# Gate and up projections by seven block products in place of eight (Strassen) in a float32 decoder trunk

## The chip, the cores and the metric

The kernel runs on one core of one Trainium2 chip. The metric is the time of one execution on the device in microseconds (us). Below, PE is the matrix engine (TensorE), PEld its weight loads, DVE the vector engine, ACT the scalar engine, POOL GpSimd and SP the engine that issues most transfers.

## The reference

A trunk of two layers works on 512 tokens of width 1024, all in float32. Each layer is a feed-forward block, a mixer block and a second feed-forward block. With `h = rmsnorm(x) * gain`, a feed-forward block is

```
x = x + 0.5 * rmsnorm((silu(h @ wg) * (h @ wu)) @ wd)      # wg, wu: 1024 x 2816, wd: 2816 x 1024
```

The mixer projects `h` with one wide matrix, runs two kinds of attention and a causal convolution on slices of it, projects and gates the three results, adds them up and multiplies by `w_out`. Its arithmetic isn't touched by the change. There are four feed-forward blocks in all (two per layer).

## The kernel before

**Precision.** Each float32 operand of a matmul is split into two parts, `hi` (ACT copies it into the type float32r, line 119) and `lo` (DVE subtracts `hi` from the value, line 120). A product is then three matmuls into the same PSUM bank: lo x hi, hi x hi and hi x lo (`mm3`, lines 137 to 139). `hh` and `hl` are the two parts of the normalised and transposed tokens, `raw` is a loaded piece of a weight.

**Gate and up (in `ffn`).** The 2816 columns of the two matrices are cut into 22 chunks of 128, `NF = 22`. For each chunk, `col_chunks` loads 256 columns of `wg` and of `wu` at a time (1 MB each, two buffers `raw`), splits them, and `proj_group` runs 8 steps of the contraction x 3 matmuls with 512 token columns for gate and the same for up. Then ACT applies silu (line 290), DVE multiplies (291), and the product is split again (293 and 294) and kept for the down projection. The first two chunks are done by `proj_lead` in two halves of 256 tokens, so that PE can begin when half of the tokens are normalised.

**Down (`proj_out`).** For two halves of 512 output columns, 22 contraction steps x 4 token tiles x 3 matmuls with 512 columns. The last steps (`tail`: 8 in the second half) are ordered by token tile, so that the first tiles are complete early and their norm and the next stage's norm (`prenorm`: norm on ACT, DVE and POOL, transposes on PE, split on ACT and DVE) run while PE works on the last tiles. The split weights of that tail go to buffers of the feed-forward block (`slots`), not to the ring `hi`/`lo`, which has `HLB = 3` buffers each.

**Order.** Dependencies and buffers are followed by a scheduler at build time. It puts each engine's instructions into a fixed order: of those that can run, the one that comes first in the program. On the chip each engine goes through its list in that order. PSUM has eight banks of 512 float32 per partition, shared out as `pm` 3, `ps` 2, `pt` 2, `po` 1.

## Time and profile before

| | |
|---|---|
| Median of 3 runs | 2572.33 us (2569.75 to 2574.19) |
| Profiled execution, time | 2571.34 us |
| Its span in the trace | 2569.5 us |
| PE matmuls | 12,072 |
| DVE busy | 1247.5 us |
| ACT busy | 930.4 us |

The span is what the trace covers; the rest of the execution's time lies around it. Matmuls are pipelined, so that the duration of one is longer than the step from one start to the next; the steps are read from the starts. Busy time of the other engines is the time in which they execute. The granted clock is a column of the profile: 1.00 means 2.4 GHz.

### The profile page before, as it was taken

Reading aid. Unit: us, or ns where it says so; the run is one execution under the profiler, and the core shown is the slowest. Engines: PE = TensorE matmul, PEld = TensorE weight load, DVE = VectorE, ACT = ScalarE, POOL = GpSimd, SP = SyncE. Lnnn points to the kernel's source line nnn. Section 1 sums busy time; section 2 is a strip of 40 time slices with the busy share of each in tenths; the row PEclk is TensorE's granted clock in tenths of the full one; section 3 lists DMA queues with packets and bytes.
Section 4 is the critical chain, followed back from the end, with each engine's and each line's share of the span. In section 5 each row is a group of like instructions: output and inputs, shape, how many; then the busy total and the mean of one; then the engine's idle time right before and its main releaser. Section 6 shows DMA issues by size and latency. Waiting matters only on the chain.

```text
span 2569.5 us, 29966 instructions
## 1 busy us (share of the span) xinstructions
PE 2521.8 (98%) x12072; PEld 2101.8 (82%) x12072; DVE 1247.5 (49%) x1838; ACT 930.4 (36%) x1625; POOL 245.7 (10%) x156
## 2 busy tenths in 40 slices
PE   8999999999999999999999999999899999999999
PEld 7888888778787888888888888887788878888887
DVE  4333244796577453332443332446956765433323
ACT  4322244633524442222332222446235244422222
POOL 0000012160011110000000000130600101100000
PEclk9999999999999999999999999999999999999999
DMA  4323345242122422223322223452421224132232
GB/s 157 103 98 98 107 147 145 65 130 93 42 91 74 165 86 97 92 92 105 107 95 92 93 98 106 157 141 59 129 80 52 91 74 165 65 99 99 99 107 74
DMA packets 211820, 261.48 MB, mean 102 GB/s; under 512 B 8160, under 2 KB 167264, under 8 KB 211424
## 3 DMA queue, kind: packets, MB, share of 16 engines
q1 hardware_dynamic: 204000, 249.06, 29.6%
q10 hardware_dynamic: 7680, 10.50, 1.6%
q8 instruction: 95, 1.56, 0.2%
q14 instruction: 45, 0.37, 0.0%
HBM read 237.47 MB, written 6.29 MB: 95 GB/s over the span
## 4 chain that ended last, share of the span: by engine, by line
PE 92%; DVE 5%; issue 1%; ACT 1%; DMA 0%; ACTq 0%; SPq 0%; DVEq 0%
PE pm L137 23%; PE pm L138 23%; PE pm L139 23%; PE ps L138 2%; PE ps L139 2%; PE ps L137 2%; DVE y L363 2%; PE pt L138 2%; PE pt L139 2%; PE pt L137 2%; PE po L137 1%; PE po L138 1%; PE po L139 1%; DVE lo L120 1%; PE pt L487 1%
## 5 line engine op out<-in xcount | busy, mean ns | idle before, releaser
L137 PE MATMUL pm<-hh,lo 128*128 128x512 f32 (+1 forms) x2288 | 869.9, 380 | 3.2 <-DVE lo L120 3.2
L138 PE MATMUL pm<-hh,hi 128*128 128x512 f32 (+1 forms) x2288 | 868.8, 380 | 0.0
L139 PE MATMUL pm<-hl,hi 128*128 128x512 f32 (+1 forms) x2288 | 867.6, 379 | 0.0
L120 DVE TENSOR_TENSOR lo<-raw,hi 128x1024 fp32r<-128x1024 f32 x374 | 486.4, 1302 | 717.0 <-ACT hi L119 715.1
L119 ACT ACTIVATE hi<-raw 128x1024 fp32r<-128x1024 f32 x374 | 395.8, 1059 | 706.8 <-PE pm L139 349.5
L137 PEld LDWEIGHTS pm<-hh,lo 128*128 128x128 f32 x2288 | 431.3, 188 | 86.2 <-DVE lo L120 5.0
L139 PEld LDWEIGHTS pm<-hl,hi 128*128 128x128 f32 x2288 | 431.3, 189 | 79.9 <-issue 0.7
L138 PEld LDWEIGHTS pm<-hh,hi 128*128 128x128 f32 x2288 | 431.3, 188 | 79.6 <-issue 0.7
L363 DVE SCALAR_TENSOR_TENSOR y<-z,ppl,y 128x512 f32<-128x512 f32 x240 | 213.5, 890 | 4.2
L291 DVE TENSOR_TENSOR sg<-sg,pm 128x512 f32<-128x512 f32 (+1 forms) x88 | 59.5, 676 | 247.6 <-PE pm L139 215.5
L290 ACT ACTIVATE sg<-pm 128x512 f32<-128x512 f32 x88 | 51.6, 591 | 327.7 <-PE pm L139 327.7
L213 POOL TENSOR_TENSOR h<-x,gain 128x512 f32<-128x512 f32 x40 | 52.4, 1331 | 1159.4 <-DVE x L271 1131.8
L137 PE MATMUL pm<-hi,il 128*128 128x512 f32 x264 | 102.7, 389 | 0.0
L138 PE MATMUL pm<-hi,ih 128*128 128x512 f32 x264 | 102.7, 389 | 0.0
L139 PE MATMUL pm<-lo,ih 128*128 128x512 f32 x264 | 102.7, 389 | 0.0
L395 POOL TENSOR_TENSOR sw<-sw,cs 128x512 f32<-128x512 f32 x40 | 64.0, 1600 | 244.1 <-DMA sw<-raw 127.2
L479 DVE CUSTOM_DVE_ANT_0 s<-ps,cs 128x256 f32<-128x256 f32 (+3 forms) x128 | 56.2, 448 | 57.1 <-ACT st L489 17.5
L616 ACT ACTIVATE gt<-pm,late 128x512 f32<-128x512 f32 x40 | 27.6, 690 | 137.3 <-PE pm L139 137.3
L636 POOL TENSOR_TENSOR m<-gt 128x512 f32<-128x512 f32 x16 | 33.6, 2103 | 408.4 <-DVE gt L623 408.4
L137 PE MATMUL pm<-hi,hl 128*128 128x512 f32 (+1 forms) x144 | 53.9, 374 | 13.7 <-DVE qk L391 13.7
L384 ACT ACTIVATE raw<-pm 128x512 f32<-128x512 f32 x40 | 23.9, 598 | 105.3 <-PE pm L139 66.1
L294 DVE TENSOR_TENSOR il<-sg,ih 128x512 fp32r<-128x512 f32 x88 | 60.3, 685 | 3.4 <-ACT ih L293 3.4
(288 smaller groups left out, 3369.1 us busy)
## 6 DMA issues: line engine op xcount, KB each, us to landing
raw<-in_w_in_dram SPq DMA_DIRECT2D x62, 1024.0 KB, 5.4
raw<-in_ffn_w_gate_dram SPq DMA_DIRECT2D x43, 1024.0 KB, 5.0
raw<-in_ffn_w_up_dram SPq DMA_DIRECT2D x43, 1024.0 KB, 5.0
raw<-in_ffn_w_down_dram SPq DMA_DIRECT2D x40, 1024.0 KB, 4.7
sw<-raw ACTq DMA_DIRECT2D x160, 64.0 KB, 2.0
raw<-in_w_out_dram SPq DMA_DIRECT2D x8, 1024.0 KB, 4.7
raw<-in_ffn_w_down_dram SPq DMA_DIRECT2D x8, 512.0 KB, 3.3
xd<-x SPq DMA_DIRECT2D x16, 256.0 KB, 2.0
```

The lines of the kernel that those rows point to most:

```text
L119: S.activation(hi, raw, AF.Copy)
L120: last = V.tensor_sub(lo, raw, bc(hi))
L137: PE.matmul(ps, sl, mh, start=first, stop=False, skip_group_check=not check)
L138: PE.matmul(ps, sh, mh, start=False, stop=False, skip_group_check=not check)
L139: PE.matmul(ps, sh, ml, start=False, stop=last, skip_group_check=not check)
L213: G.tensor_mul(h[j], xs[t][:, j * T:(j + 1) * T], g[:, j * T:(j + 1) * T])
L290: S.activation(sg[:, c], pg, AF.Silu)
L291: V.tensor_mul(sg[:, c], sg[:, c], pu)
L294: V.tensor_sub(il, sg, bc(ih))
L363: V.scalar_tensor_tensor(y, z[:, j:j + T], cw[:, c, j:j + 1], y, op0=ALU.mult, op1=ALU.add)
L395: G.tensor_mul(sw, sw, sin)
L479: V.tensor_tensor_reduce(out=s, in0=ps, in1=mask, scale=1.0, scalar=3e38, op0=ALU.add, op1=ALU.min, accum_out=nm)
```

## The change

From the second pair of chunks on (`u` = 1 to 10), the 256 columns of gate and the 256 columns of up are handled as one matrix product. The contraction (1024) is cut into two halves and the tokens into two halves of 256; "rows" are the two halves of the pair of matrices, `wg` and `wu`. A 2x2 by 2x2 block product takes eight block products, and Strassen's scheme (in Winograd's form) takes seven. Each block product, `product`, is 2 column groups x 4 contraction steps x 3 matmuls with 256 token columns. The sums and differences that the scheme needs are formed by DVE: on the weight side `s1` to `s4` in each unit, on the token side four tiles `tt` once per block, before the first unit. Partial results are combined in PSUM: ACT copies a bank that holds a partial sum into another bank (`W`, `Vb`, `Y`), and the next product adds onto it. The last product of a unit, with `s4`, is issued in the next unit (`late`). The first unit is plain (`lead_unit`, the same 192 matmuls with 256 columns as `proj_lead`).

The gated product is kept unsplit, and `proj_out` splits it for the down projection, in each of its two halves. There, `slots` is None: the tail's weights go to the ring `hi`/`lo`, whose buffers go from 3 to 4 each, and the tail of the second half is 6 steps, not 8. In the first feed-forward block four matmuls and four ACT reads (`own`) are put ahead of the lead. `hh` and `hl` become two halves of one tile `hb`. `FUSE` is False, so the branches that it guards aren't built. The scratch space for dynamic transfers is set to 1024.

```diff
--- before.py
+++ after.py
@@ -33,7 +33,8 @@
 QA0, KA0, VA0 = 0, 768, 1536
 
 TAIL = 8
-HLB = 3
+HLB = 4
+FUSE = False
 ZRB = 6
 PRE_UP = 60
 CST = [("ident", 128), ("cos", 512), ("sin", 512), ("mc", 512), ("m0", 256), ("m12", 256)]
@@ -144,6 +145,32 @@
             for k in range(KD):
                 mm3(p_, wh[:, k, :], wl[:, k, :], hh[:, k, :], hl[:, k, :], k == 0, k == KD - 1)
         return ps
+
+    def lead_unit(wg, wu, hb, raws=None):
+        if raws is None:
+            raws = [load(w[:, 0:2 * P], KD, 2 * P) for w in (wg, wu)]
+        wts = {(f, j): split(raws[j][:, :, f * P:(f + 1) * P]) for f in range(2) for j in range(2)}
+        H = T // 2
+        whole = [bank("pm") for _ in range(2)]
+        parts = [bank("pt") for _ in range(2)]
+        for s in range(2):
+            c = slice(s * H, (s + 1) * H)
+            outs = [(whole[0], c, s == 0), (whole[1], c, s == 0),
+                    (parts[s], slice(0, H), True), (parts[s], slice(H, T), False)]
+            for (f, j), (z, d, first) in zip(((0, 0), (0, 1), (1, 0), (1, 1)), outs):
+                for k in range(KD):
+                    wh, wl = (w[:, k, :] for w in wts[f, j])
+                    m = hb[:, :, k, c]
+                    PE.matmul(z[:, d], wl, m[:, 0, :], start=first and k == 0, stop=False, skip_group_check=True)
+                    if FUSE:
+                        o = z.rearrange("p (a n) -> p a n", n=H)[:, d.start // H:d.start // H + 1, :]
+                        PE.matmul(o.to_broadcast([P, 2, H]), wh, m, start=False, stop=k == KD - 1,
+                                  skip_group_check=True)
+                    else:
+                        PE.matmul(z[:, d], wh, m[:, 0, :], start=False, stop=False, skip_group_check=True)
+                        PE.matmul(z[:, d], wh, m[:, 1, :], start=False, stop=k == KD - 1, skip_group_check=True)
+        return [[(slice(0, T), *whole)],
+                [(slice(s * H, (s + 1) * H), parts[s][:, 0:H], parts[s][:, H:T]) for s in range(2)]]
 
     def proj_lead(w, c0, c1, hh, hl, spare, raws=None):
         if raws is None:
@@ -198,11 +225,11 @@
         first = g is not None
         if g is None:
             g = bcast_row(row)
-        hh = per.tile([P, KD, T], F32R, tag="hh", name="hh")
-        hl = per.tile([P, KD, T], F32R, tag="hl", name="hl")
+        hb = per.tile([P, 2, KD, T], F32R, tag="hb", name="hb")
+        hh, hl = hb[:, 0], hb[:, 1]
         with tc.high_priority(offset=PRE_UP):
             prenorm_tiles(g, hh, hl, first)
-        return hh, hl
+        return hb
 
     def prenorm_tiles(g, hh, hl, first):
         for t in range(NT):
@@ -227,22 +254,23 @@
                 S.activation(dh, pt, AF.Copy)
                 V.tensor_sub(hl[:, 4 * j:4 * j + 4, t * P:(t + 1) * P], pt, bc(dh))
 
-    def proj_out(stat, slots, w, row, half_step):
-        K = len(stat)
+    def proj_out(K, stat, ntail, slots, w, row, half_step):
         g = bcast_row(row)
         ss = [[sp.tile([P, 1], F32, tag="ss", name="ss", bufs=8) for _ in range(2)] for _ in range(NT)]
         yg = []
         for half in range(2):
             ps = [bank(b_) for b_ in (("pm", "pm", "pm", "ps") if half == 0 else ("pt", "ps", "pt", "po"))]
             c0 = half * T
-            tail = K - (2 if half == 0 else len(slots))
-            parts = {}
+            tail = K - (2 if half == 0 else ntail)
+            parts, pairs = {}, {}
             for k0 in range(0, K, 4):
                 kn = min(4, K - k0)
                 raw = load(w[k0 * P:(k0 + kn) * P, c0:c0 + T], kn, T)
                 for s in range(0, kn, 2):
                     k = k0 + s
-                    if half == 0 or k < tail:
+                    for u in range(2):
+                        pairs[k + u] = stat(k + u)
+                    if slots is None or half == 0 or k < tail:
                         wh, wl = split(raw[:, s:s + 2, :])
                         for u in range(2):
                             parts[k + u] = (wh[:, u, :], wl[:, u, :])
@@ -253,7 +281,7 @@
                 if k0 + kn == K:
                     ops += [(k, t) for t in range(NT) for k in range(tail, K)]
                 for k, t in ops:
-                    sh, sl = stat[k]
+                    sh, sl = pairs[k]
                     wh, wl = parts[k]
                     mm3(ps[t], sh[:, t * P:(t + 1) * P], sl[:, t * P:(t + 1) * P], wh, wl, k == 0, k == K - 1)
             for t in range(NT):
@@ -271,34 +299,138 @@
                     V.scalar_tensor_tensor(xs[t][:, 0:T], yg[t], r, xs[t][:, 0:T], op0=ALU.mult, op1=ALU.add)
                     V.scalar_tensor_tensor(xs[t][:, T:D], y, r, xs[t][:, T:D], op0=ALU.mult, op1=ALU.add)
 
+    def product(dst, sw, mv, start):
+        for f in range(2):
+            for k in range(4):
+                c = slice(f * P, (f + 1) * P)
+                sh, sl = sw[0][:, k, c], sw[1][:, k, c]
+                m = mv[:, :, k, :]
+                PE.matmul(dst[:, f, :], sl, m[:, 0, :], start=start and f == 0 and k == 0, stop=False, skip_group_check=True)
+                if FUSE:
+                    PE.matmul(dst[:, f:f + 1, :].to_broadcast([P, 2, T // 2]), sh, m, start=False, stop=k == 3,
+                              skip_group_check=True)
+                else:
+                    PE.matmul(dst[:, f, :], sh, m[:, 0, :], start=False, stop=False, skip_group_check=True)
+                    PE.matmul(dst[:, f, :], sh, m[:, 1, :], start=False, stop=k == 3, skip_group_check=True)
+
     def ffn(pre, post, wg, wu, wd, early=None):
         gain, raws = early or (None, None)
-        hh, hl = prenorm(pre, gain)
+        H = T // 2
+        hb = prenorm(pre, gain)
         with tc.tile_pool(name="inner", bufs=1, reuse_waits="tile") as ip:
-            inner = []
-
-            def pair(f):
-                return tuple(ip.tile([P, T], F32R, tag=f"i{u}{f}", name="i" + u) for u in "hl")
-
-            spare = iter((NF - 1, NF - 2))
-            lead = proj_lead((wg, wu), 0, 0, hh, hl, lambda: pair(next(spare)), raws)
-            rest = ([(slice(0, T), *proj_group([gc[1], uc[1]], hh, hl))]
-                    for gc, uc in zip(col_chunks(wg, 256, FF), col_chunks(wu, 256, FF)))
-            for f, pieces in enumerate(chain(lead, rest)):
-                sg = sp.tile([P, T], F32, tag="t2k", name="sg", bufs=5)
-                for c, pg, pu in pieces:
-                    S.activation(sg[:, c], pg, AF.Silu)
-                    V.tensor_mul(sg[:, c], sg[:, c], pu)
-                ih, il = pair(f)
-                S.activation(ih, sg, AF.Copy)
-                V.tensor_sub(il, sg, bc(ih))
-                inner.append((ih, il))
-                if early and f == 5:
-                    lambdas()
-            proj_out(inner, [lambda f=f: pair(f) for f in range(TAIL)], wd, post, True)
+            inner = [ip.tile([P, 2, T], F32, tag=f"i{u}", name="inner") for u in range(NF // 2)]
+            t2k = lambda name: sp.tile([P, 2, H], F32, tag="t2k", name=name, bufs=5)
+            with tc.tile_pool(name="comb", bufs=1, reuse_waits="tile") as cp:
+                def comb(name):
+                    return cp.tile([P, 4, H], F32, tag="s", name=name, bufs=4)
+
+                def block(k, t):
+                    return hb[:, :, 4 * k:4 * k + 4, t * H:(t + 1) * H]
+
+                if early:
+                    own = [bank(tag) for tag in ("pm", "pm", "pm", "po")]
+                    for z in own:
+                        PE.matmul(z, hb[:, 0, 0, 0:P], hb[:, 0, 0, :], start=True, stop=True, skip_group_check=True)
+                    for z in own:
+                        S.activation(junk[0][:, 0:1], z[:, 0:1], AF.Copy)
+                lead = lead_unit(wg, wu, hb, raws)
+
+                b = {}
+                def added(k, t):
+                    b[k, t] = comb("b")
+                    z = block(k, t)
+                    V.tensor_add(b[k, t], bc(z[:, 0]), bc(z[:, 1]))
+
+                tt = {}
+                def tsplit(i, z):
+                    tt[i] = cp.tile([P, 2, 4, H], F32R, tag=f"t{i}", name="t")
+                    split(z, (tt[i][:, 0], tt[i][:, 1]))
+
+                fl = lambda z: z.rearrange("p a b -> p (a b)")
+                added(0, 0)
+                added(0, 1)
+                V.tensor_sub(fl(b[0, 0]), fl(b[0, 0]), fl(b[0, 1]))
+                added(1, 1)
+                V.tensor_sub(fl(b[0, 1]), fl(b[1, 1]), fl(b[0, 1]))
+                V.scalar_tensor_tensor(fl(b[1, 1]), fl(b[1, 1]), -1.0, fl(b[0, 0]), op0=ALU.mult, op1=ALU.subtract)
+                tsplit(6, b[1, 1])
+                tsplit(5, b[0, 0])
+                added(1, 0)
+                V.scalar_tensor_tensor(fl(b[1, 0]), fl(b[1, 1]), -1.0, fl(b[1, 0]), op0=ALU.mult, op1=ALU.subtract)
+                tsplit(4, b[1, 0])
+                tsplit(7, b[0, 1])
+                for f, pieces in enumerate(lead):
+                    for c, pg, pu in pieces:
+                        z = inner[0][:, f, c]
+                        S.activation(z, pg, AF.Silu)
+                        V.tensor_mul(z, z, pu)
+
+                def pbank(tag):
+                    return bank(tag, (P, 2, H))
+
+                late = []
+                for u in range(1, NF // 2):
+                    c0 = u * 2 * P
+                    rg, ru = [load(w_[:, c0:c0 + 2 * P], KD, 2 * P) for w_ in (wg, wu)]
+                    w11, w12, w21, w22 = rg[:, 0:4, :], rg[:, 4:8, :], ru[:, 0:4, :], ru[:, 4:8, :]
+                    X, W = pbank("ps"), pbank("pm")
+                    Vb, Y = pbank("pt"), pbank("pm" if u % 2 == 0 else "po")
+                    it = inner[u]
+                    s1, s2 = comb("s1"), comb("s2")
+                    o11 = split(w11)
+                    V.tensor_add(s1, w21, w22)
+                    V.tensor_add(s2, s1, w11)
+                    product(X, o11, block(0, 0), True)
+                    S.activation(W, X, AF.Copy)
+                    os2 = split(s2)
+                    for f_ in late:
+                        f_()
+                    late.clear()
+                    product(X, os2, tt[6], False)
+                    S.activation(Vb, X, AF.Copy)
+                    o12 = split(w12)
+                    s4, s3 = comb("s4"), comb("s3")
+                    V.tensor_add(s4, s2, w12)
+                    V.tensor_add(s3, w11, w21)
+                    product(W, o12, block(1, 0), False)
+                    g1 = t2k("g1")
+                    S.activation(g1, W, AF.Silu)
+                    os1 = split(s1)
+                    product(X, os1, tt[5], False)
+                    S.activation(Y, X, AF.Copy)
+                    o22 = split(w22)
+                    product(Vb, o22, tt[4], False)
+                    a2 = t2k("a2")
+                    V.tensor_copy(a2, Y)
+                    V.tensor_sub(a2, Vb, a2)
+                    os3 = split(s3)
+                    product(X, os3, tt[7], False)
+                    V.tensor_add(a2, a2, X)
+                    V.scalar_tensor_tensor(it[:, :, 0:H], a2, -1.0, g1, op0=ALU.mult, op1=ALU.mult)
+
+                    def finish(X=X, Y=Y, s4=s4, it=it, t2k=t2k):
+                        product(Y, split(s4), block(1, 1), False)
+                        g2 = t2k("g2")
+                        S.activation(g2, Y, AF.Silu)
+                        V.scalar_tensor_tensor(it[:, :, H:T], X, -1.0, g2, op0=ALU.mult, op1=ALU.mult)
+
+                    late.append(finish)
+                    if early and u == 2:
+                        lambdas()
+                late[0]()
+            with tc.tile_pool(name="pairs", bufs=1, reuse_waits="tile") as pp:
+                def stat(k):
+                    if k < 2:
+                        into = tuple(sp.tile([P, T], F32R, tag="h", name="i" + u, bufs=4) for u in "hl")
+                    else:
+                        into = tuple(pp.tile([P, T], F32R, tag="i" + u, name="i" + u, bufs=11) for u in "hl")
+                    return split(inner[k // 2][:, k % 2, :], into)
+
+                proj_out(NF, stat, TAIL - 2, None, wd, post, True)
 
     def mixer(l):
-        hh, hl = prenorm(a["mix_norm_pre"][l])
+        hb = prenorm(a["mix_norm_pre"][l])
+        hh, hl = hb[:, 0], hb[:, 1]
         xd = dram.tile([T, D], F32, tag=f"xd{l}", name="xd")
         x_out(xd)
         wi = a["w_in"][l]
@@ -676,7 +808,7 @@
         x_in(xd)
         with tc.tile_pool(name="tw", bufs=1, reuse_waits="tile") as tw:
             tails = [lambda d=d: tuple(tw.tile([P, T], F32R, tag=f"t{u}{d}", name="t" + u) for u in "hl") for d in range(TAIL)]
-            proj_out(mm, tails, a["w_out"][l], a["mix_norm_post"][l], False)
+            proj_out(KD, lambda k: mm[k], TAIL, tails, a["w_out"][l], a["mix_norm_post"][l], False)
         mrg.__exit__(None, None, None)
 
     gain0 = []
@@ -756,7 +888,7 @@
     host["cst"] = _constants()
     host["pp"] = _per_partition(i)
     host["lam"] = _lambdas(i)
-    nc = _bacc.Bacc("TRN2", target_bir_lowering=False, num_devices=1)
+    nc = _bacc.Bacc("TRN2", target_bir_lowering=False, num_devices=1, dynamic_dma_scratch_size=1024)
     arrays, aps = {}, {}
     for n, v in host.items():
         arrays[f"in_{n}_dram"] = v
```

## Rows read from the trace of the kernel before

**Rows 1.** The page: busy time, the span in 40 slices, the chain that ended last

```profile
PE 2521.8 (98%) x12072; PEld 2101.8 (82%) x12072; DVE 1247.5 (49%) x1838; ACT 930.4 (36%) x1625; POOL 245.7 (10%) x156
...
PEclk9999999999999999999999999999999999999999
...
PE 92%; DVE 5%; issue 1%; ACT 1%; DMA 0%; ACTq 0%; SPq 0%; DVEq 0%
```

**Rows 2.** Timeline of PE, gate and up, 512 columns (start, duration, engine, line)

```profile
60.00 0.39 PE L138 MATMUL pm<-hh,hi 128*128 128x512 f32 x1
...
65.89 0.39 PE L137 MATMUL pm<-hh,lo 128*128 128x512 f32 x1
```

**Rows 3.** Timeline of PE in the first block's lead, 256 columns

```profile
18.96 0.28 PE L137 MATMUL pm<-hh,lo 128*128 128x256 f32 x1
...
23.04 0.28 PE L138 MATMUL pm<-hh,hi 128*128 128x256 f32 x1
```

**Rows 4.** Groups by line and shape, gate and up, 44 to 270 us

```profile
L120 DVE TENSOR_TENSOR lo<-raw,hi 128x1024 fp32r<-128x1024 f32 x41 | 50.3, 1226 | 93.5 <-ACT hi L119 93.5
L119 ACT ACTIVATE hi<-raw 128x1024 fp32r<-128x1024 f32 x42 | 44.5, 1059 | 84.5 <-PE pm L139 67.1 <-PE ps L138 8.0 <-issue 7.9
L291 DVE TENSOR_TENSOR sg<-sg,pm 128x512 f32<-128x512 f32 x20 | 13.8, 688 | 51.2 <-PE pm L139 51.2
L294 DVE TENSOR_TENSOR il<-sg,ih 128x512 fp32r<-128x512 f32 x20 | 13.7, 685 | 0.6 <-ACT ih L293 0.6
L293 ACT ACTIVATE ih<-sg 128x512 fp32r<-128x512 f32 x20 | 12.3, 616 | 2.2 <-DVE sg L291 2.2
L290 ACT ACTIVATE sg<-pm 128x512 f32<-128x512 f32 x20 | 12.0, 601 | 72.6 <-PE pm L139 72.6
```

**Rows 5.** Groups by line and shape, whole span

```profile
L384 ACT ACTIVATE raw<-pm 128x512 f32<-128x512 f32 x40 | 23.9, 598 | 105.3 <-PE pm L139 66.1 <-DMA sw<-raw 39.1
L271 DVE SCALAR_TENSOR_TENSOR x<-yg,rstd,x 128x512 f32<-128x512 f32 x24 | 18.0, 749 | 0.6
```

**Rows 6.** Windows: length, PE, PEld, DVE, ACT, POOL busy (count), clock, DMA

```profile
18.00:22.00 4.00, 4.00 (x36) 4.00 (x35) 4.00 (x8) 2.61 (x6) 0.00 (x0) 1.00 0.32 88
44.00:267.00 223.00, 223.00 (x986) 184.65 (x985) 77.36 (x86) 66.56 (x84) 0.00 (x0) 1.00 0.29 97
1271.00:1299.20 28.20, 27.26 (x165) 23.69 (x164) 21.13 (x42) 17.98 (x44) 10.64 (x8) 1.00 0.19 61
```

**Rows 7.** DMA issues: count, KB each, median us to landing

```profile
raw<-in_ffn_w_gate_dram SPq DMA_DIRECT2D x43, 1024.0 KB, 5.0
raw<-in_ffn_w_up_dram SPq DMA_DIRECT2D x43, 1024.0 KB, 5.0
```

**Rows 8.** Timeline of one hand-over PE to ACT to DVE, mixer's lead

```profile
386.17 0.63 PE L225 MATMUL pt<-ident,h 128*128 128x128 f32 x4 [0.42 <-DVE h L222]
...
386.84 0.60 ACT L227 ACTIVATE hh<-pt 128x512 fp32r<-128x512 f32 x1 [1.93 <-PE pt L225]
...
387.47 0.69 DVE L228 TENSOR_TENSOR hl<-pt,hh 128x512 fp32r<-128x512 f32 x1 [1.05 <-ACT hh L227]
```

**Rows 9.** Timeline where the second feed-forward block hands over to the third

```profile
1288.57 0.39 PE L139 MATMUL po<-il,ih 128*128 128x512 f32 x1
...
1290.03 0.36 PE L137 MATMUL pm<-hh,lo 128*128 128x256 f32 x1
...
1298.51 0.68 DVE L228 TENSOR_TENSOR hl<-ps,hh 128x512 fp32r<-128x512 f32 x1
...
1315.14 0.40 PE L137 MATMUL pm<-hh,lo 128*128 128x512 f32 x1
```

**Rows 10.** Timeline of the first block's start

```profile
14.02 0.55 PE L137 MATMUL pm<-hh,lo 128*128 128x256 f32 x1
...
23.80 0.60 ACT L227 ACTIVATE hh<-pt 128x512 fp32r<-128x512 f32 x1 [3.05 <-PE pt L225]
```

## Prediction

> **What bounds the kernel now.** I read the page first: PE is busy 98% of the span, DVE 49%, ACT 36%, the granted clock is full in every slice, and the chain that ended last is PE for 92% [rows 1]. So PE's own pace is the thing to price, and its busy time doesn't give it (matmuls overlap); the starts in the timeline do. In gate and up there are 26 steps from 60.00 to 65.89: 0.2267 us for each matmul of 512 columns [rows 2]. The same step in the lead, with 256 columns, is (23.04 - 18.96) / 34 = 0.1200 us [rows 3]. The difference is 0.1067 us for 256 columns, which leaves about 13 ns that each matmul pays whatever its width. A reader should keep that: halving the width doesn't halve the time. Waits come next: in 44 to 267 us PE is never idle, while DVE works 77 of 223 us and ACT 67 [rows 6]. In gate and up nothing but PE counts; DVE and ACT have more than half of their time free. The executed time to start from is 2571.3 us, that is the span of 2569.5 and 1.8 around it; the median of the runs shown is 1.0 above, which I neglect.
>
> **The units on PE.** One unit before: 2 matrices x 2 column groups x 8 steps x 3 = 96 matmuls of 512 columns, 96 x 0.2267 = 21.76 us. After: 7 products x 2 x 4 x 3 = 168 matmuls of 256 columns, 168 x 0.1200 = 20.16 us. Columns fall by one eighth (2.7 us), but 72 more matmuls pay the fixed 13 ns and 1.1 us of that is lost. Saved: 1.60 us x 10 units x 4 blocks = **64.0 us**. The lead already is 192 matmuls of 256 columns and stays so.
>
> The Trainium skill, "TensorE: Matmul & The Clock Gate", section "Back-to-back issue gap", gives N/2.4 + 2.5 ns for the gap of a matmul alone, so 216 and 109 ns. By it the units would save 40 x (96 x 0.2158 - 168 x 0.1092) = 95 us. The trace has some 11 ns more at either width [rows 2, 3], and I go by the trace.
>
> **The units on DVE and ACT.** Seven splits of 1024 elements per partition take the place of four. DVE: 7 lo at 1.226, 4 sums (s1 to s4, the same form, priced by the same row) at 1.226, one copy and two sums on PSUM at 0.688 (the nearest row), two gated products at 0.75: 8.58 + 4.90 + 2.06 + 1.50 = 17.05 us [rows 4, 5]. Before it was 4 x 1.226 + 2 x (0.688 + 0.685) = 7.65. ACT: 7 x 1.059 + 3 copies and 2 silus at 0.60 = 10.4 us [rows 4, 5]. Both fit under 20.16, DVE at 85%. That a busy DVE doesn't slow PE is seen in 18 to 22 us: DVE is busy all of the time, and PE steps at 0.1200 [rows 3, 6].
>
> Three waits could still show. *The copies.* A product ends in X, ACT copies X elsewhere, and the next product into X must wait for it. The price of such a turn when it is exposed: 0.16 (a matmul of 256 columns lasts 0.28, its step is 0.12) + 0.04 (386.80 to 386.84) + 0.60 + 0.03, about 0.84 us [rows 3, 8]; no PSUM-to-PSUM copy is in the trace, so the bounds are 0.6 and 1.3 (DVE's 0.69 in place of ACT's, both hand-overs doubled). In program order another product of 24 x 0.12 = 2.88 us stands behind each of the three copies: the late product of the unit before, then W's, then Vb's. So they are covered. *The splits.* With four buffers of hi and lo they can run three products, 8.6 us, ahead; a split needs 1.06 + 1.23. *The loads.* There are still only two `raw` buffers, both used by one unit. From the landing to the release of `wu`'s buffer DVE has some 9 instructions to do (s1, s2, s4, s3, five lo): 11.0 us, plus 1.06 for a hi, plus 5.0 to land the next [rows 4, 7]: 17.1 us for a loop that may take 20.16. Inside the units I allow 0.1 us each, **+4 us** (bounds: nothing, and 0.84 in each, 34 us).
>
> **The start of each block.** The token-side tiles need all tokens: 8 sums and 4 splits, 12 x 1.226 = 14.7 us of DVE. Take the third block: the norm ends on DVE at 1299.2, the lead on PE at 1315.1 [rows 9], and the second product of unit 1, the first that needs `tt`, is due 2.9 later, at 1318.0. In between DVE must do 13.5 (one sum can come early), 1.4 for the lead's gating (two of 0.688), s1, s2 and two lo of unit 1 (4.9), and wait once for ACT (1.06): 20.9 us against 18.8. That is 2.1 late. Also unit 1 has no late product to cover its copies, so two of its turns lie open, 1.7. Sum 3.8, for three blocks and 1.7 for the first, where DVE has more time: 3 x 3.8 + 1.7 = **+13 us** (bounds 7 and 22).
>
> **The first block.** The `own` matmuls read hh for all 512 tokens, so they wait for the last tile, whose first half is there at 24.4 [rows 10]; four matmuls (0.9) and four ACT reads of one column (about 1.2, half of what 512 columns would take) later, at 26.5, the `pm` banks are free for the lead, which before began at 14.02 [rows 10]. That is 12.5 us. The two blocks of the lead that go to `pt` can run meanwhile (48 matmuls, 5.8 us, and more at the pace of the first ones, which last 0.55 and not 0.28 [rows 3, 10]). **+5 us** (bounds 2 and 12.5).
>
> **The ends.** At the end of three blocks another stage follows. With a tail of 6 the token tiles complete every 18 x 0.2267 = 4.1 us instead of 5.4. DVE's work there was 21.1 us from 1271 to 1299, less some 2 for three splits of 512 elements, so 4.8 per tile [rows 4, 6]: now it is slower than the tiles come, and the second tile is complete 2.7 us less ahead of PE's end. Before, the lead began 1.5 us after the last matmul [rows 9]. The ring `hi`/`lo` also is held by the tail until then, so the next lead's splits come later. **+2.5 us** x 3 = **+7.5** (bounds 0 and 12). At the very end no stage follows: nothing.
>
> **Costed at nothing.** The down projection's extra 44 splits of 512 elements per block (0.62 on ACT, 0.69 on DVE [rows 4]) lie beside 12 x 0.2267 = 2.7 us of PE per step; with the weights' share DVE has 1.3 of those 2.7. Uncovered they'd be some 30 us a block. The larger ring in the mixers and the scratch space: nothing waits for them.
>
> **Sum.** 2571.3 - 64.0 + 4 + 13 + 5 + 7.5 = 2536.8, **2537 us**. All low bounds together give 2516, all high ones 2588.
>
> **Rivals.**
> *The turns are exposed (slower).* If the build's order puts a product right behind the copy that it waits for, a unit loses 0.84 for each. For: ACT and DVE run their lists in order, and a copy that ACT meets too early also holds its splits. Against: the 2.88 us of other work behind each copy. It decides from (2571.3 - 2537) / 40 = 0.86 a unit, one exposed turn. With one the time is 2570, with two 2537 + 67 = 2604.
> *DVE or the load loop becomes the bound.* DVE's 17.05 leaves 3.1 us a unit for waits on ACT and PE, and the lo's long waits for hi (93.5 us in 44 to 270 us [rows 4]) are harmless today only because DVE is half idle. If a unit takes 21.8 on DVE or by the loads, the gain is gone: 2537 + 64 = 2601. Against: the load loop has 3 us of slack, and the splits run ahead.
> *The 256-column step doesn't hold over 168 matmuls.* At 0.1295 us the unit is 21.76 again: 2601. Against: the step is even over the lead's 23 us [rows 3].
> *PE steps faster than in the lead.* Two of three matmuls use the same weights; if the fixed 13 ns fell to 2.5, the units would save 31 more: 2506. Against: the lead has that same pattern. By the section named above, the gap would be that; the trace disagrees.
>
> **Chances.** Forecast 0.71, with a range of its own of 2518 to 2556; one exposed turn a unit 0.08 (about 2570, both sides of the old time); two or more 0.07; DVE or loads 0.08; a longer step 0.03; a shorter one 0.03. A measurement tells 0.2%, 5 us, from no change. Faster: 0.71 + 0.03 + 0.06 of the partly exposed cases = 0.80; within 0.2%: 0.05; slower: 0.15. The range of 2514 to 2580 takes in the partly exposed turns and leaves out the full losses above and the shorter step below.
>
> **What would show it.** PE steps of 0.120 and a unit of 20.2 us with no idle; PE with 12,072 + 40 x 72 + 4 = 14,956 matmuls; DVE near 1247 + 40 x 9.4 + 4 x 14.7 + 176 x 0.69, some 1800 us (71%), ACT near 1205. At each block's start PE waits of 2 to 5 us for `tt` or for a copy; in the first 30 us a wait for `own`. I'd be wrong in size if the waits at the starts are several times this, and in sign if PE waits on ACT's copies or on lo in every unit.

## The result, and the profile after

The changed kernel takes 2541.23 us (median of 4, 2539.58 to 2545.07) against 2572.35 for the kernel before: a ratio of 0.9882 [0.9865, 0.9899]. Forecast were 2537 us and a range of 2514 to 2580. The profiled execution has a span of 2538.3 us, 31.2 less than before.

The page of the changed kernel, its busy line and its chain that ended last, to be read beside [rows 1]:

```profile
PE 2470.0 (97%) x14956; PEld 2194.7 (86%) x14956; DVE 1732.8 (68%) x2354; ACT 1175.3 (46%) x1953; POOL 246.6 (10%) x156
...
PE 86%; DVE 9%; ACT 2%; DMA 2%; issue 1%; SPq 0%; DVEq 0%; ACTq 0%
```

PE still sets the end, but DVE's share of the chain has grown from 5% to 9%, and DMA's from 0 to 2%: there are now places where PE waits. The matmuls are the 14,956 that were forecast.

The timeline of PE, from the first matmul into `pt` in one unit to the same one in the next:

```profile
185.43 0.28 PE L308 MATMUL pt<-t,lo 128*128 128x256 f32 x1
...
205.59 0.28 PE L308 MATMUL pt<-t,lo 128*128 128x256 f32 x1
```

Start to start, a unit is 20.16 us, 168 x 0.1200, to the hundredth. The window from 122 to 142 us (length; busy time of PE, PEld, DVE, ACT, POOL with counts; clock; DMA share; GB/s), to be read beside [rows 6]:

```profile
122.00:142.00 20.00, 20.00 (x169) 20.00 (x169) 15.79 (x17) 9.83 (x12) 0.00 (x0) 1.00 0.32 102
```

PE has no idle time there, and DVE is busy for 79%. So the gain of a steady unit is whole. The rest of the account comes from the starts of matmuls in the two traces (us, after less before). The units of the first block begin here:

```profile
49.92 0.28 PE L308 MATMUL ps<-hb,lo 128*128 128x256 f32 x1
```

| Part | after - before | forecast |
|---|---|---|
| Until the units begin, first block (40.70, now 49.92) | +9.2 | +5 |
| Units to down's first matmul: four times 217.63, now 204.62, 206.46, 204.90, 206.38 | -48.2 | -64 + 4 + 13 = -47 |
| Lead of the third block (25.11, now 31.54) | +6.4 | part of +7.5 |
| The two leads behind the mixers | -0.5 | part of +7.5 |
| Down, first to last matmul, four times | +2.0 | 0 |
| Mixers and the rest | -0.1 | 0 |
| Sum | -31.2 | -34.5 |

**The first block's start.** The timeline of PE when `own` runs (L333), to be read beside [rows 10]:

```profile
22.61 1.09 PE L252 MATMUL pt<-ident,h 128*128 128x128 f32 x4 [2.91 <-DVE h L247]
23.35 0.56 PE L164 MATMUL pt<-hb,lo 128*128 128x256 f32 x1
23.71 0.41 PE L170 MATMUL pt<-hb,hi 128*128 128x256 f32 x1
...
24.63 1.63 PE L333 MATMUL pm<-hb 128*128 128x512 f32 x3
26.06 0.63 PE L333 MATMUL po<-hb 128*128 128x512 f32 x1
26.49 0.41 PE L164 MATMUL pm<-hb,lo 128*128 128x256 f32 x1
```

The lead's part for `pm` starts at 26.49, where 26.5 was forecast and 14.02 was before. Of the 48 matmuls of the lead's first part for `pt`, which the forecast let run meanwhile, only two stand ahead of `own` (23.35 and 23.71). Before them PE waits 2.91 us for the last token tile.

**The start of the units in a later block.** Timeline of PE and DVE in the second block (in brackets the idle time before, and what ended it):

```profile
945.89 0.70 DVE L121 TENSOR_TENSOR il<-inner,ih 128x512 fp32r<-128x512 f32 x1
945.89 0.28 PE L308 MATMUL ps<-hb,lo 128*128 128x256 f32 x1
...
946.84 1.22 DVE L382 TENSOR_TENSOR s<-s,raw 128x1024 f32<-128x1024 f32 x1
...
947.98 0.69 DVE L121 TENSOR_TENSOR il<-inner,ih 128x512 fp32r<-128x512 f32 x1
...
949.71 1.22 DVE L121 TENSOR_TENSOR lo<-s,hi 128x1024 fp32r<-128x1024 f32 x1
...
951.08 0.36 PE L308 MATMUL ps<-t,lo 128*128 128x256 f32 x1 [2.15 <-DVE lo L121]
```

Unit 1 starts at 945.89. After its first product the second waits 2.15 us for the `lo` of `s2`. The reader should see the two `il` lines: they are the splits of the first two gated tiles for the down projection, some 200 us before they are used. DVE's list has them ahead of that `lo` (949.71).

**The handover to the third block.** Timeline of PE, DVE and ACT, to be read beside [rows 9]:

```profile
1273.96 1.06 ACT L120 ACTIVATE hi<-raw 128x1024 fp32r<-128x1024 f32 x1 [0.61 <-PE po L139]
...
1275.21 1.93 DVE L121 TENSOR_TENSOR lo<-raw,hi 128x1024 fp32r<-128x1024 f32 x1
...
1275.55 0.38 PE L164 MATMUL pm<-hb,lo 128*128 128x256 f32 x1 [0.84 <-ACT hb L254]
...
1277.07 0.68 DVE L255 TENSOR_TENSOR hb<-pt,hb 128x512 fp32r<-128x512 f32 x1
...
1277.80 0.58 PE L171 MATMUL pm<-hb,hi 128*128 128x256 f32 x1 [1.51 <-DVE hb L255]
```

ACT's `hi` for a weight of the next lead starts only when a matmul of the tail (`po`, L139) is through, 0.61 us of waiting. The `lo` behind it, recorded with 1.93 us, stands on DVE ahead of the tokens' `hb`, and PE waits 1.51 us for that `hb`. Later it waits 1.90 more (1287.33, for `h`).

### The profile page after: what moved, and what is told of

It reads as the page before. It is cut to its first block, busy times and chain, and to the rows that moved or that the text cites. A ratio compares the mean times of both kernels' runs of the same rounds, so it can differ in the third digit from the quotient of the medians.

```text
span 2538.3 us, 36895 instructions
## 1 busy us (share of the span) xinstructions
PE 2470.0 (97%) x14956; PEld 2194.7 (86%) x14956; DVE 1732.8 (68%) x2354; ACT 1175.3 (46%) x1953; POOL 246.6 (10%) x156
## 3 DMA queue, kind: packets, MB, share of 16 engines
q8 instruction: 118, 1.93, 0.3%
## 4 chain that ended last, share of the span: by engine, by line
PE 86%; DVE 9%; ACT 2%; DMA 2%; issue 1%; SPq 0%; DVEq 0%; ACTq 0%
PE pm L138 11%; PE pm L139 11%; PE pm L140 11%; PE ps L308 6%; PE ps L314 6%; PE ps L313 6%; PE pm L308 2%; PE pm L313 2%; PE pm L314 2%; PE ps L139 2%; PE ps L140 2%; DVE lo L121 2%; PE ps L138 2%; PE pt L140 2%; PE pt L138 2%; PE pt L139 2%
## 5 line engine op out<-in xcount | busy, mean ns | idle before, releaser
L138 PE MATMUL pm<-hb,lo 128*128 128x512 f32 (+1 forms) x848 | 325.1, 383 | 0.0
L139 PE MATMUL pm<-hb,hi 128*128 128x512 f32 (+1 forms) x848 | 324.2, 382 | 0.0
L140 PE MATMUL pm<-hb,hi 128*128 128x512 f32 (+1 forms) x848 | 323.6, 382 | 0.0
L308 PE MATMUL ps<-t,lo 128*128 128x256 f32 x960 | 273.0, 284 | 10.9 <-DVE lo L121 6.5
L314 PE MATMUL ps<-t,hi 128*128 128x256 f32 x960 | 272.2, 284 | 0.0
L313 PE MATMUL ps<-t,hi 128*128 128x256 f32 x960 | 272.2, 284 | 0.0
L121 DVE TENSOR_TENSOR lo<-s,hi 128x1024 fp32r<-128x1024 f32 x160 | 195.2, 1221 | 68.9 <-ACT hi L120 68.9
L120 ACT ACTIVATE hi<-s 128x1024 fp32r<-128x1024 f32 x160 | 164.7, 1051 | 96.2 <-DVE s L382 94.9
L308 PEld LDWEIGHTS ps<-t,lo 128*128 128x128 f32 x960 | 184.7, 192 | 12.5 <-ACT hi L120 7.0
L138 PEld LDWEIGHTS pm<-hb,lo 128*128 128x128 f32 x848 | 159.6, 188 | 31.8 <-issue 1.8
L140 PEld LDWEIGHTS pm<-hb,hi 128*128 128x128 f32 x848 | 159.5, 188 | 30.0 <-issue 0.7
L139 PEld LDWEIGHTS pm<-hb,hi 128*128 128x128 f32 x848 | 159.5, 188 | 30.0 <-issue 0.7
L314 PEld LDWEIGHTS ps<-t,hi 128*128 128x128 f32 x960 | 184.8, 193 | 0.0
L313 PEld LDWEIGHTS ps<-t,hi 128*128 128x128 f32 x960 | 184.8, 193 | 0.0
```

The costliest lines, as they stand in the source:

```text
L120: S.activation(hi, raw, AF.Copy)
L121: last = V.tensor_sub(lo, raw, bc(hi))
L138: PE.matmul(ps, sl, mh, start=first, stop=False, skip_group_check=not check)
L139: PE.matmul(ps, sh, mh, start=False, stop=False, skip_group_check=not check)
L140: PE.matmul(ps, sh, ml, start=False, stop=last, skip_group_check=not check)
L308: PE.matmul(dst[:, f, :], sl, m[:, 0, :], start=start and f == 0 and k == 0, stop=False, skip_group_check=True)
```

## Experiments

Each edit but the first is on the changed kernel.

**Half-width matmuls without Strassen** (on the kernel before: the units' matmuls in two halves of 256 tokens).

```diff
-            for k in range(KD):
+            for c in (slice(0, T // 2), slice(T // 2, T)) if narrow else ():
+                for k in range(KD):
+                    mm3(p_[:, c], wh[:, k, :], wl[:, k, :], hh[:, k, c], hl[:, k, c], k == 0, k == KD - 1, check=False)
+            for k in range(KD) if not narrow else ():
```

`narrow` is True for the units alone.

> The kernel before, with the units' matmuls cut to 256 columns (first half of the tokens, then the second), and nothing else changed: 192 matmuls a unit in place of 96. Theory (each matmul pays about 13 ns whatever its width): a unit takes 192 x 0.1200 = 23.04 us in place of 21.76, 40 units are 51 us more, 2572 + 51 = 2623 us. Rival (the gap of a lone matmul, 109 and 216 ns): 192 x 0.1092 = 20.97 against 96 x 0.2158 = 20.72, 10 us more, 2582 us.

Measured: 2620.81 us, ratio 1.0184 [1.0167, 1.0201]. Its PE timeline:

```profile
59.82 0.28 PE L137 MATMUL pm<-hh,lo 128*128 128x256 f32 x1
59.94 0.28 PE L138 MATMUL pm<-hh,hi 128*128 128x256 f32 x1
60.06 0.28 PE L139 MATMUL pm<-hl,hi 128*128 128x256 f32 x1
```

The step is 0.12 and the ten units of a block take 230.40 us, 10 x 192 x 0.1200. The same columns in twice as many matmuls cost 48.5 us, so the fixed 13 ns per matmul is paid at both widths. The formula that the Trainium skill ("TensorE: Matmul & The Clock Gate", section "Back-to-back issue gap") has for the gap of a matmul alone, 216 and 109 ns, would give an estimate of about 10 us and some 2582; this stream, with a weight load for every matmul, doesn't follow it.

**No late product** (the seventh product is issued in its own unit).

```diff
-                    late.append(finish)
+                    finish()
...
-                late[0]()
```

> The changed kernel with the last product of a unit (s4) issued at the end of its own unit, not inside the next one. Theory (each copy out of X needs another product behind it, and an exposed turn costs 0.84 us): nothing stands between product 1, the copy and product 2 any more, and a unit after the first loses 0.84 (36 units, 30 us, about 2571 us), or 1.7 if the second copy is laid open too (61 us, about 2602). Rival (the build's order puts another product between by itself): the time stays at 2541 us within 5.

Measured: 2568.27 us (ten runs, 2561.08 to 2575.66), ratio 0.9984 [0.9969, 0.9998]: 27 us dearer than the change as made. The turn that is now open, in the timeline of PE and ACT:

```profile
157.46 0.28 PE L314 MATMUL ps<-hb,hi 128*128 128x256 f32 x1
...
157.78 0.58 ACT L384 ACTIVATE pm<-ps 128x512 f32<-128x512 f32 x1 [1.33 <-PE ps L314]
...
158.41 0.39 PE L308 MATMUL ps<-t,lo 128*128 128x256 f32 x1 [0.67 <-ACT pm L384]
```

From 157.46 to 158.41 are 0.95 us in place of 0.12: the turn costs 0.83 (0.84 was forecast), and 0.1 more at the next step (0.22). Each unit from the second on takes 21.08 us in place of 20.16, one open turn more. So a copy between two PSUM banks takes 0.58 us, and the order of the products hides it.

**Two more sums of DVE on the load buffers.**

```diff
                     V.tensor_add(s3, w11, w21)
+                    V.tensor_add(s3, w11, w21)
+                    V.tensor_add(s3, w11, w21)
```

> The changed kernel with one weight sum (s3, 1024 elements) formed three times in each unit, so two more DVE instructions of 1.14 to 1.23 us, with the same result. Theory (in the units PE sets the pace, DVE works 15.8 of each 20.2 us and has 4 to spare): DVE goes to 18.1, the units still step at 20.16, and the time rises by no more than 10 us, most of it at the blocks' starts (2541 to 2551 us). Rival (DVE's order is the bound already and its waits are not slack): each extra instruction shows in full, 2.3 x 40 = 92 us, 2633 us.

Measured: 2608.77 us, ratio 1.0139 [1.0115, 1.0163]. The theory fell: 2.4 us of DVE a unit cost 67 us, 1.7 a unit. The issues of the two loads, and DVE:

```profile
146.04 0.37 SPq L128 DMA_DIRECT2D raw<-in_ffn_w_gate_dram  x1
...
147.14 0.85 SPq L128 DMA_DIRECT2D raw<-in_ffn_w_up_dram  x1
...
155.49 1.23 DVE L381 TENSOR_TENSOR s<-raw 128x1024 f32<-128x1024 f32 x1 [1.36 <-DMA raw<-in_ffn_w_up_dram]
```

The reads of both buffers now end close together, the loads are issued 1.1 us apart, and here the second lands 8.3 us after its issue. That is one of the longest: the 34 loads of `up` that go out so close behind those of `gate` take 6.7 to 8.6 us, with a median of 6.9. (In the changed kernel the two are mostly 3.8 apart and the median of both is 5.0.) DVE, with time to spare, waits for the load here, and PE for ACT's copies behind it.

DVE waits like this for the load of `up` in ten of the 40 units. Most of the others take 21.4 to 21.6 us, and that can be read off the load of `gate` alone:

```profile
168.92 0.37 SPq L128 DMA_DIRECT2D raw<-in_ffn_w_gate_dram  x1
...
190.40 0.37 SPq L128 DMA_DIRECT2D raw<-in_ffn_w_gate_dram  x1
```

From issue to issue are 21.48 us: 5.20 to land, and 16.28 until DVE has read the buffer for the last time. In the changed kernel it is 5.11 and 15.05, 20.16 in all (175.99 to 196.15). The two sums put 2.3 us more into the loop, and it gets 1.3 longer, so it had about 1 us to spare.

**The same DVE work away from the load buffers** (the `lo` of `s3` is written three times).

```diff
                     os3 = split(s3)
+                    V.tensor_sub(os3[1], s3, bc(os3[0]))
+                    V.tensor_sub(os3[1], s3, bc(os3[0]))
```

> The changed kernel with two more DVE instructions of 1024 elements in each unit, as in the run with s3 formed three times, but such that hold no load buffer: the lo of s3 is formed three times, with the same result. In the run with s3 the time rose by 67 us, against at most 10 expected. Theory now (the loop of the two load buffers binds: landing, sums, release, next landing; its slack is under 1 us and not 3, and two loads issued within 1.1 us of each other land in 8 us and not 5): the same 2.3 us of DVE work away from the release of the buffers costs less than a third of that, 2541 to 2561 us. Rival (DVE's total work and its order bind, wherever the work stands): about 67 us again, 2608 us.

Measured: 2539.80 us, ratio 0.9878 [0.9861, 0.9896]: nothing. These two instructions stand behind the last read of the buffers. So it wasn't DVE's total that cost 67 us, but how long it holds `raw`. The load loop is the near bound, and DVE isn't.

**`own` from the first token tile** (the moving operand is the first tile at four contraction steps, so that the four matmuls need one tile and not all).

```diff
-                        PE.matmul(z, hb[:, 0, 0, 0:P], hb[:, 0, 0, :], ...
+                        PE.matmul(z.rearrange("p (k n) -> p k n", n=P), hb[:, 0, 0, 0:P], hb[:, 0, 0:4, 0:P], ...
```

> The changed kernel with the four matmuls ahead of the first lead reading the first token tile alone (128 tokens x 4 contraction steps, the same 512 columns) and not all 512 tokens. Theory (the lead's start at 26.5 us in place of 14.0 is the wait of these four for the last tile, 9.5 us later at the lead's end): the lead begins at 14 to 15 us, its end comes back to 41 to 43 us, and 7 to 9 us are gained, 2533 us. Rival (the lead would wait anyway, for the raw weights or for DVE, now busier with the token tiles): less than 2 us.

Measured: 2533.30 us, ratio 0.9848 [0.9833, 0.9863]. The lead starts at 13.97 (14.02 before) and the units at 40.79, 9.1 earlier; the first block's units then take 207.98 in place of 204.62, and 3.4 are given back: 1.5 by a longer wait in unit 1 (2.15 in place of 0.67), and 1.5 by a granted clock of 0.50 right behind it (16 matmuls in the 3.2 us from 47.3). The profiled runs are 7.0 apart; the 1.2 that are left aren't in one place. The third lead is 1.3 shorter and the fourth block's units 1.5, both where the granted clock fell once more in the changed kernel's profile than in this one; other stages differ the other way.

**The tail: its length, and where its weights are.** A 2 x 2 of the tail (6 or 8 steps) and the place of its split weights (the ring, or `inner`'s buffers that the tail has done with).

```diff
-                proj_out(NF, stat, TAIL - 2, None, wd, post, True)
+                def slot(f):
+                    z = ip.tile([P, 2, T], F32R, tag=f"i{f}", name="tw")
+                    return z[:, 0], z[:, 1]
+                proj_out(NF, stat, 8, [lambda f=f: slot(f) for f in range(8)], wd, post, True)
```

> The changed kernel with the end of the feed-forward blocks as before: a tail of 8 steps in the second half of the down projection, whose split weights go to the gate and up block's own tiles that are free by then, not to the ring of hi and lo. Theory (the lead after the second block loses 6 us since the tail's shape or its hold on the ring makes the norms late): the lead of the third block goes from 31.5 us back to 25, the other blocks' leads (24.8) stay, and the time falls by 5 to 7 us, 2535 us. Rival (the lead's wait comes from something else, the token sums on DVE): no change within 2 us.

> As the run before it, but with the tail of 6 kept, only its weights moved out of the ring. If the ring is the cause (the next lead's splits wait for buffers that the tail holds, and then stand among the norms on DVE), the lead of the third block is at 25 to 27 us. If the shorter tail is (tiles complete every 4.1 us, DVE needs 4.8), it stays at 30 to 32.

> The changed kernel with a tail of 8 in place of 6, its weights in the ring as in the changed kernel, so that all four buffers are held. If the ring is the cause, the lead of the third block gets longer than 31.5 us, by 2 or more, and the mixers' leads too. If the shorter tail is, it falls to 25 to 27.

| Weights, tail | third lead, us | time, us |
|---|---|---|
| ring, 6 (the change) | 31.54 | 2541.23 |
| ring, 8 | 28.77 | 2537.38 (one run) |
| own buffers, 6 | 26.35 | 2528.40 (one run) |
| own buffers, 8 | 24.83 | 2528.45, ratio 0.9827 [0.9811, 0.9844] |

By the table the ring costs the third lead 5.2 us at a tail of 6 and 3.9 at 8; the shorter tail costs 2.8 and 1.5. Each lead is from one profile, though, and the first row holds more than the ring: the granted clock falls twice within that lead, and once in the second row's. In four other runs that leave the tail and its weights as in the change it falls once, and the lead takes 30.2 to 30.3 us. With 30.2 the table comes out even: 3.9 for the ring at either length, 1.4 and 1.5 for the shorter tail, and 1.3 for the fall that only the first row has. A longer tail in the ring didn't make the lead longer still: that theory fell. With own buffers and a tail of 8 this lead takes what the others do. The lead explains 6.7 of the 12.8 us of the last row. In the profiled runs, which are 11.2 apart, the second mixer is 3.7 shorter and down 0.3 in three of the blocks. The waits of PE for `wl` at the leads of the two mixers (1.48 and 2.19 us in the changed kernel) are gone in both runs with own buffers; but the second mixer differs by 6.5 us among the profiles of this study (543.9 to 550.4), and I can't say how much of the 3.7 the edit did.

**The early splits put off** (the first two pairs of gated tiles are split into buffers of the down projection's own pool, as the others, and not into the norm's `h` buffers, which are free once the norm is through).

```diff
-                    if k < 2:
-                        into = tuple(sp.tile([P, T], F32R, tag="h", name="i" + u, bufs=4) for u in "hl")
-                    else:
-                        into = tuple(pp.tile(...) for u in "hl")
+                    into = tuple(pp.tile(...) for u in "hl")
```

> The changed kernel with all 22 split tiles of the down projection taken from the pool that opens after the units, so that the splits of the first two (0.69 each on DVE, 0.62 on ACT) can't be done at the block's start any more. Theory (unit 1's second product waits 2.3 us for the lo of s2, and those two splits stand ahead of it on DVE and ACT): the wait falls by about 1.4 us in each block, 4 to 6 us in all, 2536 us, unless the down projection's start waits for them (1 us a block at most). Rival (the chain of the token sums alone sets the wait, or the load's landing): the wait stays within 0.5 us, 2541 us.

Measured: 2529.67 us, ratio 0.9841 [0.9825, 0.9858], 11.6 us against the change as made, twice what was expected. The wait in unit 1 of the second block falls from 2.15 to 1.06:

```profile
948.43 0.35 PE L308 MATMUL ps<-t,lo 128*128 128x256 f32 x1 [1.06 <-DVE lo L121]
```

The four blocks' units take 204.57, 204.47, 203.93 and 203.98, 5.4 less in all, of which 1.5 are a stretch of the fourth block at the lower clock that this profile doesn't have. Down takes 1.4 less. A wait that I hadn't counted goes too. The waits of PE in the changed kernel (total, times, longest):

```profile
PE ps L308 <- DVE lo L121: 6.5, 3, 2.2
PE ps L308 <- ACT pm L384: 4.4, 5, 1.7
PE pm L138 <- DVE wl L121: 3.7, 2, 2.2
```

and in this one:

```profile
PE ps L308 <- ACT pm L384: 5.1, 6, 1.8
...
PE ps L308 <- DVE lo L121: 2.1, 2, 1.1
```

The wait for `wl`, 3.7 us at the leads of the two mixers, is no longer listed. As it is gone with the tail's own buffers too, both edits are credited with it.

**The token-side sums on POOL** (`added` by GpSimd, four sums a block taken from DVE).

```diff
-                    V.tensor_add(b[k, t], bc(z[:, 0]), bc(z[:, 1]))
+                    G.tensor_add(b[k, t], bc(z[:, 0]), bc(z[:, 1]))
```

> The changed kernel with the four sums of hi and lo on the token side done by POOL, not by DVE. Theory (DVE's chain of 21 us sets the wait at unit 1): DVE is relieved of 4.9 us at each start, but POOL takes about 2.0 to 2.6 us for 1024 elements (it takes 1.3 for 512) and three of them stand in the chain, so the chain is about as long: the wait of 2.3 us changes by less than 1.5 either way. If DVE's load and not the chain's length sets the wait, the wait is gone (9 us less in all).

Measured: 2552.94 us (one run), 12 dearer. Neither forecast held: the units of the three later blocks take 206.9 to 208.7 us, the leads of the second and fourth block 27.70 in place of 24.83. PE's waits for ACT's copies into `pm` grow from 4.4 to 11.8 us. DVE has less to do there and PE waits longer; that the sums are a chain whose later links need the earlier, slower ones is what I take it to be, and wasn't tried by itself.

**The three that gained, together** (`own` from one tile, own buffers and a tail of 8, early splits put off).

> The changed kernel with the four first matmuls on the first token tile, the tail of 8 outside of the ring and the late splits, together. Theory (three separate waits at three places): the gains add up, 9 at the first block's lead less the 1 to 2 that its first unit gives back, 7 or more at the third block's lead, and what the late splits give by themselves: 2541 - 8 - 9 - 4 = 2520 us, within 6.

Measured: **2515.14 us** (2513.92 to 2516.40), ratio **0.9781 [0.9766, 0.9795]** against the kernel before. It beats both kernels, by 56 us and by 26, and lies within the 6 us of its forecast. The gains don't add up in full, as the theory had it: one by one they were 7.9, 12.8 and 11.6, which is 32.3. The wait for `wl` is in two of them. Its page:

```profile
PE 2461.2 (98%) x14956; PEld 2189.1 (87%) x14956; DVE 1734.4 (69%) x2370; ACT 1178.6 (47%) x1969; POOL 243.8 (10%) x156
```

The lead starts at 14.06, the units at 40.42, and the three leads behind take 24.84 each. Of the units, 206.09, 204.99, 204.31 and 203.81 us, some 3.2 each over 201.6 are left: waits of 1.1 to 1.7 at the start and an open turn.

## Why the prediction was right

**The units** (-64.0): exact. 20.16 us each, against 21.76 (by the rows, fewer columns take 2.56 off and the fixed parts put 0.96 on; the working had 2.7 and 1.1); the first experiment shows that the step's fixed part is what holds the gain at 1.6 a unit.

**Inside the units and at their starts** (+4 and +13): 16.0 measured (822.4 for the four blocks less 40 x 20.16 = 806.4), 13.1 at the starts (1.0, 4.0, 3.3 and 4.8) and 2.9 in two steady units, one of the first block and one of the second, with waits of 1.75 and 0.64 us. The step for the starts was right in mechanism and size: `lo` of `s2` was forecast 2.1 late and PE waits 2.15. Of the two open turns in unit 1, one shows, and in unit 2 (0.92). The fourth block also has 1.5 us at the lower clock behind the wait, which weren't forecast. And the 13.5 of DVE's work that I counted wasn't the whole: the early splits, which I had put into the down projection, stand there as well, and putting them off gave 5.4 us over the four blocks, 1.5 of it by the clock.

**The turns** (0.84 if open, hidden by the products behind them): right, by the second experiment. Without the late product the change would be worth 4 us in place of 31.

**The first block's own** (+5): mis-sized, 9.2. The time of 26.5 was right, and the bounds of 2 to 12.5 held; the step that failed is that the `pt` blocks of the lead hide more than half of the 12.5 us. They hid next to nothing, two matmuls of 48. The 3.3 us that came back have another reason: the lead before took 26.7 us, among the transposes of the last two token tiles and with its first 15 matmuls at steps of 0.21 and more, and the late one takes 23.4 (26.49 to 49.92). Undoing the wait gave 9.1 at this place and 7.9 in all.

**The ends** (3 x 2.5): 5.9 measured, so the sum was near, but not for its reasons, and that is luck. At the two ends before a mixer the times hardly change; what shows is at the one before the third block. There the ring, which I had named in a half sentence, is worth 3.9, the shorter tail, on which the sum was built, 1.5, and one of the two falls of the clock 1.3. In the mixers two things cancel: the changed kernel waits 3.7 us for `wl`, which the kernel before doesn't, and the kernel before waits 3.2 for the `lo` of a weight, which the changed one doesn't. Whether the larger ring took the latter away wasn't tried.

**Costed at nothing**: down took 2.0 us more in all, 484.2 in place of 482.2 for the four blocks from the first matmul to the last. It is 482.8 with the early splits put off, 483.4 with a tail of 8 in either place, and 482.0 with the three edits together, so these two account for it. The lower clock was no term of the sum either (the digit 9 of the page, read as full, is 90% or more). It cost 2.4 us in the third lead and 1.5 in the fourth block.

**The total** is 4 us off because the errors are small and partly cancel: 4 too little for the first block and 2 for down, against 1 and 2 too much for the units' starts and the ends.

**The rivals.** "DVE or the load loop becomes the bound" was judged against by 3 us of slack in the load loop. That step failed without showing much in the time. The load of `up` and what DVE does between its landing and its release, in the changed kernel:

```profile
179.82 0.37 SPq L128 DMA_DIRECT2D raw<-in_ffn_w_up_dram  x1
...
185.53 1.22 DVE L381 TENSOR_TENSOR s<-raw 128x1024 f32<-128x1024 f32 x1
...
198.72 1.23 DVE L121 TENSOR_TENSOR lo<-raw,hi 128x1024 fp32r<-128x1024 f32 x1 [0.26 <-ACT hi L120]
...
199.98 0.37 SPq L128 DMA_DIRECT2D raw<-in_ffn_w_up_dram  x1
```

The load takes 5.0, and `s1` reads it from 185.53: at most 0.7 us lie between. From there to the release are 14.4 us, where the forecast had 12.1 (nine instructions and one `hi`): DVE's copy, the two sums on PSUM and the two gated products stand in its list between them. That is where most of the 3 us went. 2.4 us more on the buffers put the kernel 36 us over the one before. The working also took the landing as 5.0 however the loads fall; it has a median of 6.9 when the two are close. Once the loop shows in the changed kernel itself: in the first block two loads go out late and 0.5 apart (77.37 and 77.91), ACT waits 1.88 for the first of them, and that unit takes 22.15. The chance of 0.08 was low for a bound that near. DVE's 17.05 us a unit was somewhat high (15.8 of 20 in the window above): it adds up durations of 1.23, and back to back these instructions start 1.14 apart (193.73, 194.87 and 196.00). DVE's total was no danger.

For the rival of a faster step, 31 us holds if the kernel before were faster too. Its time was measured, and with 0.1092 in the changed kernel alone the units would save 40 x 168 x 0.0108 = 73 more, some 2464. For the rival of a longer step, [rows 3] show 4 of the lead's us and not 23.

## What to carry to other kernels

Price fewer, narrower matmuls by the step from the starts at each width, not by columns: here an eighth fewer columns gave 7.4% per unit. A product that accumulates onto a copied bank needs other work of PE behind the copy, and here one product held over to the next unit is enough. With few load buffers, count how long each is held, from its landing to its last read in the engine's list, and not only how busy the engine is. Where a scheduler fills a list with whatever can run, early free buffers pull work of a later stage ahead of what is urgent: which buffers come free, and when, is part of the schedule.

## What the runs showed of the hardware

Two loads of 1 MB issued at most 1.1 us apart, in the run with two more sums: the second landed after 6.7 to 8.6 us, with a median of 6.9, where the median of loads issued 3.8 apart is 5.0 (the changed kernel).

The granted clock isn't full everywhere in the changed kernel. Two windows in the third lead:

```profile
1276.90:1280.20 3.30, 2.40 (x11) 2.40 (x12) 3.30 (x9) 1.36 (x6) 1.37 (x1) 0.55 0.53 167
...
1287.10:1290.50 3.40, 3.17 (x16) 3.20 (x17) 1.86 (x5) 1.20 (x2) 0.00 (x0) 0.56 0.17 66
```

Ahead of them PE had been idle for 0.84 and 1.51 us, and for 1.90. Inside, the steps of 256 columns are 0.213 and not 0.120 (1278.18 to 1279.88: 8 steps), which is the level of 1.2 GHz in place of 2.4. From 1277.80 to 1280.71 thirteen matmuls take 2.91 us in place of 1.56, and from 1288.80 to 1291.01 ten take 2.21 in place of 1.20. That is 2.4 us on top of the waits.

The same wait doesn't always bring it about. In unit 1 of the third and of the fourth block PE waits 2.15 us for `lo`; the windows behind these two waits:

```profile
1312.30:1315.70 3.40, 3.40 (x28) 3.40 (x29) 3.40 (x4) 1.68 (x3) 0.00 (x0) 1.00 0.04 8
2212.60:2215.80 3.20, 3.20 (x17) 3.20 (x17) 2.81 (x3) 0.48 (x1) 0.00 (x0) 0.50 0.41 120
```

The unit takes 19.66 us in the third block and 21.14 in the fourth. So a short wait can cost 1.5 us more than its length, and not in every block. Among the ten runs of the kernel with no late product the mean granted clock is 0.994 and 0.995 in the two shortest (2561.08 and 2561.61) and 0.990 in the two longest (2573.50 and 2575.66 us).
